# One square of softmax weights per query block: adding the two key blocks of a sliding window before the transposes and parting them with a mask behind

## The chip, the cores and the metric

The kernel runs on one core of a Trainium2 chip. A core has a matrix engine (TensorE, called PE in the profile, with its weight loads on a line of their own, PEld), a vector engine (VectorE, DVE), an engine for activation functions (ScalarE, ACT), a general engine (GpSimd, POOL), and a queue engine (SyncE, SP) that issues most of the DMA transfers here. The metric is the time of one execution on the device in microseconds (us); less is better.

## What is computed

The program is a decoder of two layers on 512 tokens of width 1024, in float32. Layer A has latent attention with 8 heads, layer B has attention in a sliding window of 128 tokens with 16 query heads and 4 key/value heads. Each layer ends with an MLP of width 4096 with a squared ReLU, and both halves end in a layer norm. The part that the change touches is the mixer of layer B:

```python
def _swa(x, w_q, sinks, w_o, k_band, v_band, rel_bias):
    q = (x @ w_q).reshape(B, nb, BLOCK, SWA_KV_HEADS, G, SWA_HEAD_DIM)
    s = jnp.einsum('bnqkgd,bnjkd->bnkgqj', q, k_band).astype(jnp.float32) * SWA_HEAD_DIM ** -0.5
    i = jnp.arange(BLOCK)
    j = jnp.arange(2 * BLOCK)
    dist = i[:, None] + BLOCK - j[None, :]
    ...
    valid = (dist >= 0) & (dist < WINDOW)
    ...
    s = jnp.where(mask[None, :, None, None], s + bias, -jnp.inf)
    ...
    p = jnp.exp(s - m[..., None])
    denom = p.sum(-1) + jnp.exp(sink - m)
    p = (p / denom[..., None]).astype(x.dtype)
    o = jnp.einsum('bnkgqj,bnjkd->bnqkgd', p, v_band).reshape(B, S, SWA_Q_HEADS * SWA_HEAD_DIM)
    return o @ w_o
```

A block of 128 queries sees two blocks of keys, the one before it and its own. With the window of 128, query i of a block sees of its own block the keys up to i, and of the block before the keys after i. So of each pair (query, position in a block) exactly one of the two key blocks has a weight, and the other has zero. The first query block has no block before it.

## The kernel before

Every float32 product is made from two parts: `split` copies a tile to a rounded high part (ACT) and subtracts that from the tile for a low part (DVE, or POOL where the call says so), and matrix products add the terms high by high, high by low and low by high. `group` issues matmuls into one PSUM bank; `bank()` takes one of six banks under the tag `mm`, and `tbank()` one of two under `tr` for transposes. `pe(...)` pins an instruction to the order of the program on its engine; all matmuls and transposes are pinned, so PE's order is that of the code. The other engines' instructions are ordered by the framework's scheduler ahead of the run, and each engine then works through its list in that order. A tile with a tag and `bufs=n` shares n rooms with the other tiles of the tag; a new one waits until an old one has been read for the last time.

Layer B goes through 16 units, one per head, in `run_steps`, with the scores two heads ahead (`AHEAD_B`). In step u PE is given: the scores of head u + 2, some work of the list `fill` (query projections of later heads, in halves; values of blocks 2 and 3; parts of the output projection), the transposes of head u (`turn`), and the mix of head u - 1 (`mix`). For one head:

- `scores`: 8 matmuls for the four query blocks into two banks; DVE adds the bias and takes the row maxima (L1408) and makes the shift `nb` (L1412).
- `weigh`: ACT makes four exponentials with row sums (L1424) and the sink's (L1428); DVE adds them and takes the reciprocal `ri` (L1429, L1430); POOL multiplies the weights by it, first the 128 columns of query block 0, then the 768 of the other three (L1431, L1433). For heads 12 to 14 `weigh` is put off into `turn`.
- `turn`: seven transposes of 128x128 (L1444 and L1446), four of own key blocks and three of the blocks before, into two banks, and two splits into `pth` and `ptl` (512 and 384 columns).
- `mix`: 8 matmuls into one bank: for each key block the values, 64 high and 64 low columns side by side in `vv`, with the weights of that block's own queries and of the next block's, 256 columns (128 for the last). ACT copies the lower half of the bank (L1477), DVE adds it to the upper one (L1478), and after the second head of a pair the pair's output `o` is split into `oh` and `ol`, the low part on POOL.

POOL also makes the low parts of six of the eight `w_sq` weight tiles and of `w_so` tiles 0, 1, 2, 6 and 7 (`wl`). The pool `gp` has one room, tag `gb`; before the change the last two `w_so` tiles are fetched into it ahead of their use (`fetch_two`).

Of the kernel before, what the change touches and what calls it, by code (L numbers as in the profile page):

```python
# [8 lines left out]
F32 = mybir.dt.float32  # L9
# [39 lines left out]
def build(tc, nc, io, out):  # L49
    with ExitStack() as top:  # L50
# [368 lines left out]

        ident = cp.tile([P, P], F32, name="ident")  # L420
# [537 lines left out]
        with tc.tile_pool(name="mla", bufs=1) as mp:  # L958
# [3 lines left out]
            cmask = const[:, C_MASK : C_MASK + 512]  # L962
            cos = const[:, C_COS : C_COS + 256].rearrange("p (t d) -> p t d", t=NT)
# [263 lines left out]
            def turn(h, i):  # L1227
# [62 lines left out]
        def fetch_two(i):  # L1290
            room = gp.tile([P, 2, 1024], F32, tag="gb", bufs=1, name=nm("raw2"))
            for j in range(2):
                fetchers[i + j](room[:, j, :])

        fetch_two(first_o + 6)
# [11 lines left out]
        with tc.tile_pool(name="swa", bufs=1) as mp:  # L1307
# [13 lines left out]
            vv = mp.tile([P, NT, SKVH, P], F32R, name="vv")  # L1321
            wv = []

            vb = {}

# [12 lines left out]
            def values_out(t):  # L1338
                split(vv[:, t, :, 0:64], vv[:, t, :, 64:P], vb[t].rearrange("p (j d) -> p j d", j=4))
# [43 lines left out]
            pts = [None] * SQH  # L1383
# [36 lines left out]
            def weigh(h, bs, nb, sm, ri):  # L1420
                p = mp.tile([P, NT, 256], F32, tag="p", bufs=3, name=nm("p"))
                for n in range(NT):
                    lo_c = P if n == 0 else 0
                    state["exp"] = nc.scalar.activation(  # L1424
                        p[:, n, lo_c:], bs[n // 2][:, n % 2, lo_c:], AF.Exp, bias=nb[:, n : n + 1],
# [5 lines left out]
                nc.gpsimd.tensor_mul(p[:, 0, P:], p[:, 0, P:], ri[:, 0:1].broadcast_to([P, P]))  # L1431
                rest = ri[:, 1:].unsqueeze(2).broadcast_to([P, NT - 1, 256])
                nc.gpsimd.tensor_mul(p[:, 1:, :], p[:, 1:, :], rest)  # L1433
                ps_of[h] = p

            def turn(h, _):
                p = ps_of[h]
                pth = mp.tile([P, NT, 256], F32R, tag="pth", bufs=2, name=nm("pth"))
                ptl = mp.tile([P, NT, 256], F32R, tag="ptl", bufs=2, name=nm("ptl"))
                for k2 in range(2):  # L1440
                    pt = tbank().rearrange("p (a b) -> p a b", a=2)
                    for a in range(2):
                        kb = 2 * k2 + a
                        pe(nc.tensor.transpose(pt[:, a, 0:P], p[:, kb, P:256], ident))  # L1444
                        if kb + 1 < NT:
                            pe(nc.tensor.transpose(pt[:, a, P:256], p[:, kb + 1, 0:P], ident))  # L1446
                    if k2 == 0:

                        with behind((state["exp"],) if h < 10 else None):
                            split(pth[:, 0:2, :], ptl[:, 0:2, :], pt)  # L1450
                    else:
                        flat = lambda z: z.rearrange("p a b -> p (a b)")
                        c = slice(512, 512 + 384)
                        split(flat(pth)[:, c], flat(ptl)[:, c], flat(pt)[:, 0:384])
                pts[h] = pth, ptl
                if waiting:
                    weigh(*waiting.pop())

            ob = [None] * 8

            def mix(h):
                m, a, j = h // 2, h % 2, h // GRP
                if a == 0:
                    ob[m] = mp.tile([P, S], F32, tag="o", bufs=2, name=nm("o"))
                o = ob[m]
                pth, ptl = pts[h]

                b = bank()
                for kb in range(NT):
# [150 lines left out]
```

## Time and profile before

| | |
|---|---|
| median of 3 runs | 993.04 us (993.04 to 993.51) |
| the profiled execution's own time | 993.19 us |
| its span, first to last instruction | 991.4 us |
| granted clock of TensorE | 0.999 of full speed |
| PE busy in the span | 985.3 us (99%) |
| DVE, ACT, POOL busy | 772.2, 555.1, 222.5 us |
| transposes of layer B's weights | 112 (64 at L1444, 48 at L1446), 549.5 to 626.0 us |

The profile is of one execution. A row of its groups names the line of the code, the engine, the operation, what is written and read (tiles by name, without numbers), the shape as partitions x elements, the count, the busy time in us and the mean of one in ns, and then the idle time of that engine just before these instructions and who ended it. The chain of waits follows the work that ended last back from the end; a piece of it is given with its start, its length and the number of instructions. Most of the kernel's matmuls carry the line of the helper `group` (L105) and most splits those of `split` (L77 for the high part, L81 for the low part), so they are told apart by the tiles.

### The profile page before, as it was taken

Reading aid. Unit: us, or ns where it says so; the run is one execution under the profiler, and the core shown is the slowest. Engines: PE = TensorE matmul, PEld = TensorE weight load, DVE = VectorE, ACT = ScalarE, POOL = GpSimd, SP = SyncE. Lnnn points to the kernel's source line nnn. Section 1 sums busy time; section 2 is a strip of 40 time slices with the busy share of each in tenths; the row PEclk is TensorE's granted clock in tenths of the full one; section 3 lists DMA queues with packets and bytes.
Section 4 is the critical chain, followed back from the end, with each engine's and each line's share of the span. In section 5 each row is a group of like instructions: output and inputs, shape, how many; then the busy total and the mean of one; then the engine's idle time right before and its main releaser. Section 6 shows DMA issues by size and latency. Waiting matters only on the chain.

```text
span 991.4 us, 15829 instructions
## 1 busy us (share of the span) xinstructions
PE 985.3 (99%) x6107; PEld 888.3 (90%) x6107; DVE 772.2 (78%) x1240; ACT 555.1 (56%) x851; POOL 222.5 (22%) x207
## 2 busy tenths in 40 slices
PE   9999999999999999999999999999999999999998
PEld 9888888998899999998898998889998998999986
DVE  6589858989768769786686778798885986898756
ACT  5557644467547547646146789536763663664620
POOL 0231101121312212210002775412121122023000
PEclk9999999999999999999999999999999999999999
DMA  7421236399889978964132213338997896898332
GB/s 262 143 90 43 93 121 201 55 230 219 147 195 231 167 163 232 221 108 147 66 107 96 86 66 139 106 85 145 255 199 123 234 213 117 224 261 146 83 128 85
DMA packets 60678, 149.55 MB, mean 151 GB/s; under 512 B 5259, under 2 KB 10300, under 8 KB 60604
## 3 DMA queue, kind: packets, MB, share of 16 engines
q0 software_dynamic: 24320, 58.73, 33.6%
q1 hardware_dynamic: 36140, 89.56, 26.5%
q8 instruction: 48, 0.79, 0.3%
q10 hardware_dynamic: 144, 0.26, 0.1%
q14 instruction: 26, 0.21, 0.1%
HBM read 146.41 MB, written 4.22 MB: 152 GB/s over the span
## 4 chain that ended last, share of the span: by engine, by line
PE 98%; DVE 1%; ACT 1%; DMA 0%; POOL 0%; issue 0%; DVEq 0%; POOLq 0%
PE mm L105 89%; PE tr L105 5%; PE tr L1236 1%; PE tr L1444 1%; PE tr L740 1%; PE tr L1446 1%; DMA raw<-in_w_qr 0%; PE tr L505 0%; ACT wh L77 0%; POOL wl L81 0%; PE mm L1144 0%; PE tr L1004 0%; DVE wl L81 0%; DVE x L479 0%; ACT vh L77 0%
## 5 line engine op out<-in xcount | busy, mean ns | idle before, releaser
L105 PE MATMUL mm<-wh,fac 128*128 128x512 f32 (+1 forms) x944 | 292.5, 386 | 0.0
L77 ACT ACTIVATE wh<-wq 128x1024 fp32r<-128x1024 f32 x164 | 173.7, 1061 | 185.0 <-PE mm L105 132.7
L81 DVE TENSOR_TENSOR wl<-wq,wh 128x1024 fp32r<-128x1024 f32 x164 | 199.5, 1221 | 67.5 <-ACT wh L77 66.6
L105 PE MATMUL mm<-xth,wh 128*128 128x256 f32 (+1 forms) x928 | 243.4, 290 | 0.0
L105 PE MATMUL mm<-xth,wl 128*128 128x256 f32 (+1 forms) x800 | 233.2, 292 | 0.0
L105 PEld LDWEIGHTS mm<-wh,fac 128*128 128x128 f32 x944 | 176.2, 188 | 35.5 <-DVE fac L81 0.6
L105 PE MATMUL mm<-xtl,wh 128*128 128x256 f32 (+1 forms) x672 | 197.1, 293 | 0.0
L105 PE MATMUL mm<-wl,fac 128*128 128x512 f32 (+1 forms) x472 | 182.3, 386 | 0.0
L105 PEld LDWEIGHTS mm<-xth,wh 128*128 128x128 f32 x928 | 168.6, 192 | 3.2
L105 PEld LDWEIGHTS mm<-xth,wl 128*128 128x128 f32 x800 | 153.2, 192 | 2.6
L77 ACT ACTIVATE wh<-raw 128x1024 fp32r<-128x1024 f32 (+3 forms) x86 | 84.9, 989 | 89.8 <-PE mm L105 61.8
L105 PEld LDWEIGHTS mm<-xtl,wh 128*128 128x128 f32 x672 | 128.7, 192 | 3.0
L204 POOL DMA_DIRECT2D wq<-in_up x64 | 77.6, 1241 | 200.3 <-DVE wl L81 193.0
L105 PEld LDWEIGHTS mm<-wl,fac 128*128 128x128 f32 x472 | 88.8, 188 | 16.6
L81 DVE TENSOR_TENSOR wl<-raw,wh 128x1024 fp32r<-128x1024 f32 (+2 forms) x64 | 75.8, 1193 | 31.3 <-ACT wh L77 31.0
L204 POOL DMA_DIRECT2D wq<-in_down x48 | 42.0, 874 | 189.1 <-DVE wl L81 183.2
L81 POOL TENSOR_TENSOR wl<-raw,wh 128x1024 fp32r<-128x1024 f32 (+2 forms) x22 | 46.8, 2130 | 89.7 <-ACT wh L77 67.2
L105 PE MATMUL mm<-wh,oh 128*128 128x512 f32 x128 | 50.8, 397 | 0.0
L105 PE MATMUL mm<-wl,oh 128*128 128x512 f32 x128 | 50.1, 391 | 0.1
L105 PE MATMUL mm<-wh,ol 128*128 128x512 f32 x128 | 50.1, 392 | 0.0
L441 POOL TENSOR_TENSOR rs<-mv,half 128x1 f32<-128x1 f32 x16 | 8.8, 553 | 168.1 <-DVE mv L486 163.4
L639 DVE TENSOR_TENSOR x<-mm,x 128x512 f32<-128x512 f32 (+1 forms) x49 | 32.9, 675 | 15.7 <-PE mm L105 15.6
(233 smaller groups left out, 1823.8 us busy)
## 6 DMA issues: line engine op xcount, KB each, us to landing
wq<-in_up POOLq DMA_DIRECT2D x64, 512.0 KB, 7.4
wq<-in_down POOLq DMA_DIRECT2D x48, 512.0 KB, 7.1
wq<-in_up SPq DMA_DIRECT2D x32, 512.0 KB, 5.5
raw<-in_down SPq DMA_DIRECT2D x28, 512.0 KB, 6.4
wq<-in_down SPq DMA_DIRECT2D x24, 512.0 KB, 6.3
raw<-in_up SPq DMA_DIRECT2D x16, 512.0 KB, 4.3
raw<-in_w_o SPq DMA_DIRECT2D x8, 512.0 KB, 3.3
raw<-in_w_sq SPq DMA_DIRECT2D x8, 512.0 KB, 3.2
```

Source lines behind the costliest of these rows:

```text
L77: high = nc.scalar.activation(dst_h, src, AF.Copy)
L81: low = (engine or nc.vector).tensor_sub(dst_l, src, f32(dst_h))
L105: pe(nc.tensor.matmul(dst, st, mv, start=first and i == 0, stop=last and i == len(pairs) - 1, **kw))
L204: state["added", key, a, more, jp] = nc.gpsimd.dma_start(half(a, jp), chunk(*more, jp), accum_op=ALU.add)
L441: state["rs"] = nc.gpsimd.tensor_tensor(r, v, half, ALU.pow)
L639: nc.vector.tensor_add(xs[t][:, c], b, xs[t][:, c])
L740: pe(nc.tensor.transpose(pt[:, a, :], xs[t][:, k * P : (k + 1) * P], ident))
L1236: pe(nc.tensor.transpose(pt[:, kb * P : (kb + 1) * P], p[:, kb * P : (kb + 1) * P], ident))
L1444: pe(nc.tensor.transpose(pt[:, a, 0:P], p[:, kb, P:256], ident))
L1446: pe(nc.tensor.transpose(pt[:, a, P:256], p[:, kb + 1, 0:P], ident))
```

## The change

In `weigh` the exponentials are laid out in seven squares of 128 columns, and POOL adds the square of the block before to the own square of query blocks 1 to 3 and then multiplies the four squares by `ri`. `turn` makes four transposes into one bank and one split of 512 columns; then POOL multiplies the high part and DVE the low part of blocks 1 to 3 by a triangular mask `tri`, which leaves the weights of the own block (`pmh`, `pml`). The two heads of a pair lie side by side.

`mix` runs once for a pair. Since the whole square is own plus before, the output of a query block is the values of the block before times the whole square, plus the difference of the own block's values and those before (`dv`) times the masked square. For query blocks 0 and 1 together that is one product with `vv` of block 0, 512 columns wide. In all there are 12 matmuls for a pair, into two banks, and four additions instead of two. `values_out` makes `dv` with three copies, three subtractions and three more splits, and drops the last split of `vv`. The mask is made in layer A from the causal mask: one operation of DVE, one transpose and one copy of ACT.

The masked squares have one room, `gb` of the pool `gp`; the two `w_so` tiles that were fetched there go to a room of the tag `xt`. The part (1, 2) of the output projection moves from step 15 to behind the last transposes. The diff, without the lines that only move:

```diff
+                if (h, i) == (2, 0):
+                    nc.vector.tensor_scalar(causal, cmask[:, 384:512], -1.0, 1.0, ALU.max, ALU.add)
...
+                if (h, i) == (4, 0):
+                    pe(nc.tensor.transpose(pt[:, 384:512], causal, ident))
+                    nc.scalar.activation(tri, pt[:, 384:512], AF.Copy)
...
-            vv = mp.tile([P, NT, SKVH, P], F32R, name="vv")
+            vv, dv = [mp.tile([P, NT - 1, SKVH, P], F32R, name=nm("vv")) for _ in range(2)]
...
             def values_out(t):
-                split(vv[:, t, :, 0:64], vv[:, t, :, 64:P], vb[t].rearrange("p (j d) -> p j d", j=4))
+                heads_of = lambda z: z.rearrange("p (j d) -> p j d", j=4)
+                own = vb[t]
+                if t + 1 < NT:
+                    split(vv[:, t, :, 0:64], vv[:, t, :, 64:P], heads_of(own))
+                    vb[t] = room[t]
+                    nc.scalar.activation(vb[t], own, AF.Copy)
+                if t > 0:
+                    d = room[3]
+                    nc.vector.tensor_sub(d, own, vb[t - 1])
+                    split(dv[:, t - 1, :, 0:64], dv[:, t - 1, :, 64:P], heads_of(d))
...
-                nc.gpsimd.tensor_mul(p[:, 0, P:], p[:, 0, P:], ri[:, 0:1].broadcast_to([P, P]))
-                rest = ri[:, 1:].unsqueeze(2).broadcast_to([P, NT - 1, 256])
-                nc.gpsimd.tensor_mul(p[:, 1:, :], p[:, 1:, :], rest)
+                nc.gpsimd.tensor_add(p[:, 2::2, :], p[:, 2::2, :], p[:, 1::2, :])
+                nc.gpsimd.tensor_mul(p[:, 0::2, :], p[:, 0::2, :], ri.unsqueeze(2).broadcast_to([P, NT, P]))
...
             def turn(h, _):
+                m, a = h // 2, h % 2
                 p = ps_of[h]
...
+                if a == 0:
+                    whole = [mp.tile([P, NT, 2, P], F32R, tag=tag, bufs=2, name=nm(tag)) for tag in ("pth", "ptl")]
+                    part = gp.tile([P, 2, NT, 2, P], F32R, tag="gb", bufs=1, name=nm("pm"))
+                    pts[m] = whole + [part[:, i, 1:] for i in range(2)]
+                pth, ptl, pmh, pml = [z[:, :, a, :] for z in pts[m]]
+                pt = tbank().rearrange("p (a b) -> p a b", a=NT)
+                for n in range(NT):
+                    pe(nc.tensor.transpose(pt[:, n, :], p[:, 2 * n, :], ident))
+                with behind((state["exp"],) if h < 10 else None):
+                    split(pth, ptl, pt)
+                own = tri[:, None, :].broadcast_to([P, NT - 1, P])
+                nc.gpsimd.tensor_mul(pmh, f32(pth[:, 1:, :]), own)
+                nc.vector.tensor_mul(pml, f32(ptl[:, 1:, :]), own)
...
+                for n2 in range(2):
+                    b = bank()
+                    parts = b.rearrange("p (n a q) -> p n a q", n=2, a=2)
+                    n = 2 * n2
+                    if n == 0:
+                        group(b, both(vv[:, 0], pth[:, 0:2], ptl[:, 0:2]), True, False, skip_group_check=True)
+                    else:
+                        for i in range(2):
+                            group(
+                                parts[:, i], both(vv[:, n + i - 1], pth[:, n + i], ptl[:, n + i]),
+                                i == 0, False, skip_group_check=True,
+                            )
+                    for i in range(1 if n == 0 else 0, 2):
+                        group(
+                            parts[:, i], both(dv[:, n + i - 1], pmh[:, n + i - 1], pml[:, n + i - 1]),
+                            False, i == 1, skip_group_check=True,
+                        )
+                    low = mp.tile([64, 2, 2, P], F32, tag="low", bufs=2, name=nm("low"))
+                    nc.scalar.activation(low, parts[hi], AF.Copy)
+                    for a, to in enumerate((lo, hi)):
+                        nc.vector.tensor_add(
+                            o[to, n2, :].rearrange("p (n q) -> p n q", n=2),
+                            parts[lo, :, a, :], low[:, :, a, :],
+                        )
...
-            for t, kp, u in (..., (0, 2, 15), (1, 2, 15), (2, 2, 16)):
+            for t, kp, u in (..., (0, 2, 15), (1, 2, 16), (2, 2, 16)):
...
-            run_steps([(h, 0) for h in range(SQH)], AHEAD_B, scores, turn, mix, fill, 1, 1, [])
+            run_steps([(h, 0) for h in range(SQH)], AHEAD_B, scores, turn, mix, fill, 2, 1, [])
```

With `per` = 2 in the last line, `run_steps` calls `mix` in every second step, after the transposes of an even head, for the pair before it.

More of the change, by code (lines that the diff above doesn't have):

```diff
@@ L1436, in turn @@
             def turn(h, _):
+                m, a = h // 2, h % 2
                 p = ps_of[h]
[L1438 to L1454, printed above, removed]
```

47 lines of the change are left out of this document (19 added, 28 removed).

## The prediction

> **What bounds the kernel now.** I read the page first, then the windows over layer B, then the chain of waits there, and then the groups by shape and the timelines of the engines that the change loads.
>
> ```profile
> span 991.4 us, 15829 instructions
> ...
> PE 985.3 (99%) x6107; PEld 888.3 (90%) x6107; DVE 772.2 (78%) x1240; ACT 555.1 (56%) x851; POOL 222.5 (22%) x207
> ```
>
> TensorE (PE) is busy for 99% of the span, and the chain of waits through layer B, below, is PE's own line from piece to piece. Its order is fixed, so every microsecond (us) of PE work that goes is a gain, and every wait of PE is a loss, one for one. The heads of layer B's attention are turned and mixed from about 550 to 626 us; this is the window of four of them in the middle:
>
> ```profile
> core 0: us, PE busy (x) PEld busy (x) DVE busy (x) ACT busy (x) POOL busy (x), PEclk, DMA share, GB/s
> ...
> 581.20:602.77 21.57, 21.57 (x142) 19.40 (x141) 16.95 (x62) 18.99 (x56) 14.61 (x13) 1.00 0.33 107
> ```
>
> In 21.57 us these four heads take 5.39 us each: PE full, ACT 4.75 us per head, DVE 4.24, POOL 3.65. PE is the limit here too, but the others are far closer to it than the 78, 56 and 22% of the page say.
>
> ```profile
> 550.55 3.69 PE mm L105 x20
> ...
> 586.59 0.11 PE tr L1444
> ...
> 587.35 4.63 PE mm L105 x28
> ...
> 602.77 0.11 PE tr L1444
> ...
> 611.76 1.88 PE mm L105 x16
> 613.63 0.11 PE tr L1444
> ```
>
> On the chain a head is seven transposes in 0.76 us (586.59 to 587.35), 0.109 each, and then matmuls. 28 of these are the mix (8), the next scores (8) and 12 of 512 columns; 16 are mix and scores alone. So the 12 cost 4.63 - 1.88 = 2.75 (0.229 each). 20 are scores and those 12: 3.69 - 2.75 = 0.94 for the scores, and 1.88 - 0.94 = 0.94 for the mix, 0.1175 a matmul, although two of its eight have only 128 columns.
>
> **The change, part by part.**
>
> PE. Three transposes fewer per head: 48 x 0.109 = 5.23 us. The mix of two heads was 16 matmuls, 1.88 us; it becomes 2 of 512 columns and 10 of 256, the same columns in fewer instructions: 2 x 0.229 + 10 x 0.1175 = 1.63. Eight pairs save 2.0. The transpose that turns the mask adds 0.11. PE path: -7.1 us, -0.45 a head, so a head takes 4.94 instead of 5.39 if nobody makes PE wait. The bound below is 5.1, should the matmuls of 128 columns not be the dear ones.
>
> ```profile
> L1433 POOL TENSOR_TENSOR p<-p,ri 128x768 f32<-128x768 f32 x16 | 23.5, 1467 | 0.0
> ...
> L1408 DVE CUSTOM_DVE_ANT_0 mm<-mm,bias 128x256 f32<-128x256 f32 x48 | 20.5, 427 | 1.6
> L81 POOL TENSOR_TENSOR wl<-raw,wh 128x1024 fp32r<-128x1024 f32 x8 | 19.2, 2405 | 5.9 <-PE mm L105 3.0 <-ACT wh L77 2.8
> ...
> L1478 DVE TENSOR_TENSOR o<-mm,low 64x512 f32<-64x512 f32 x16 | 10.9, 680 | 2.3 <-ACT low L1477 2.1
> ...
> L81 POOL TENSOR_TENSOR ol<-o,oh 128x512 fp32r<-128x512 f32 x7 | 9.0, 1285 | 3.6 <-ACT oh L77 3.6
> ...
> L81 DVE TENSOR_TENSOR ptl<-tr,pth 128x384 fp32r<-128x384 f32 x16 | 8.8, 549 | 0.0
> ...
> L1431 POOL TENSOR_TENSOR p<-p,ri 128x128 f32<-128x128 f32 x16 | 6.4, 400 | 26.5 <-DVE ri L1430 15.1 <-PE tr L1446 6.4 <-ACT pth L77 4.0
> ```
>
> These groups of layer B by shape (count, busy us, mean ns of one, idle time before) give the prices on the other engines.
>
> ACT loses the second of two splits a head, of 384 columns, and falls below its 4.75 us. The mix's copies keep their count and size.
>
> POOL. Now 0.40 + 1.47 = 1.87 a head. After: an add of 384, a multiply of 512 by the reciprocal, and a multiply of 384 by the mask. Multiplying by the reciprocal costs (1.467 - 0.400)/640 = 1.67 ns an element; two full operands cost (2.405 - 1.285)/512 = 2.19 ns with 0.165 us fixed. By the dearer rate the add and the mask cost 1.01 each, by the cheaper 0.83; I take 1.01, since both read two full operands like `ol`. With 1.04 for the middle one that is 3.06, +1.19, and POOL needs 3.65 + 1.19 = 4.84 of 4.94 us: it is nearly full where weights are split as well.
>
> DVE. It loses 0.549, and gains `pml`, 384 elements with both operands in SBUF. In PSUM that shape is 0.549, and I take 0.55. The two adds of 64x512 in a pair become four of 64x256, at 0.427 by the 256 row: 1.71 for 1.36, +0.17 a head (bounds 0 and 0.34). Together 4.24 - 0.55 + 0.55 + 0.17 = 4.41, before waits. But a two-operand SBUF instruction of DVE is held up by POOL:
>
> ```profile
> L1429 DVE TENSOR_TENSOR sm<-sm,ri x16: 156/163/1620, 541.2 to 619.5; 128x4 f32<-128x4 f32 x16
> 547.78 1.62 DVE L1429 TENSOR_TENSOR sm<-sm,ri 128x4 f32<-128x4 f32 x1 [1.37 <-ACT ri L1428]
> 546.97 2.41 POOL L81 TENSOR_TENSOR wl<-raw,wh 128x1024 fp32r<-128x1024 f32 x1
> ```
>
> An addition of four columns, 0.163 us in the median, once took 1.62 and ended at 549.40, when POOL's 2.41 us instruction did (549.38). In the old loop this tiny one is DVE's only operation of that kind; `pml` is a second and larger one, beside a POOL that hardly rests. The Trainium skill, SBUF — State Buffer, section "Who interferes with whom", has it as a rule: a DVE instruction with two SBUF inputs and a GpSimd instruction that reads SBUF exclude each other, and the later one blocks. The trace agrees in those three rows.
>
> The values: five more ACT and five more DVE instructions of 256 columns (three copies and three subtractions, with one split less of `vv` and three of `dv`), 2.1 us on DVE by the 0.427 row. Half run before the loop, half in its first step, and `dv` is needed only at the first mix, 8 us later: nothing, or up to 2.1 if that step were full. The mask in layer A is two small operations under PE work: nothing.
>
> Moves. The two loads of 512 KB for `w_so` go to an `xt` room free once the last query has read `x2`; they keep their place on SP's queue and their weights are used only behind the loop: nothing. The part (1,2) behind the last transposes covers the last masks: nothing. The mask's one buffer makes POOL's and DVE's masks of an even head wait for the mix of the pair before, which follows that head's transposes on PE by 1.6 us; behind them queue the next weights on POOL and the next scores' bias on DVE. The split that feeds these masks follows the same transposes, so the wait is at most those 1.6 us, for masks that PE needs only a pair later: nothing.
>
> Where PE will wait. POOL's room is the time from its weights to their transposes:
>
> ```profile
> 596.69 1.47 POOL L1433 TENSOR_TENSOR p<-p,ri 128x768 f32<-128x768 f32 x1
> ...
> 611.89 1.47 POOL L1433 TENSOR_TENSOR p<-p,ri 128x768 f32<-128x768 f32 x1
> ```
>
> Head 10 is weighed by 598.16 and turned at 602.77 (the chain, above): 4.6 us of room. With 4.84 of its own and 0.55 in which `pml` holds it up, POOL loses 5.39 - 4.94 = 0.45 us a head, some 3.6 over heads 2 to 9. The room is just used up: I take 0.6 us of stall. In heads 10 to 13 a PE step is shorter (611.76 to 613.63 is mix and scores alone). There `ol` of heads 6 and 7 must come out between the weights, one such instruction late: 1.2. Head 13 was weighed at 613.36 for transposes at 613.63, 0.27 us of room; from its scores PE now comes 2 x 0.327 + 0.25 = 0.90 sooner, the weighing takes 0.19 more, and half to a whole mask is ahead of it: 0.8 to 1.8, taken as 1.5.
>
> The PSUM banks are the other place:
>
> ```profile
> 577.30 0.27 PE L105 MATMUL mm<-skh,q 128*128 128x128 f32 x1
> ...
> 584.27 0.30 ACT L1428 ACTIVATE ri<-nb,sink 128x4 f32<-128x4 f32 x1
> ```
>
> ```profile
> PEld mm L105 <- ACT p L1424: 0.2, 1, 0.2
> ```
>
> Of six, the scores of two heads need four, the mix now two at once, the queries one or two. A head's scores free theirs 7.0 us after their start (577.30 to 584.27), and PE comes for the next after 0.94 + 2.75 + 0.44 + 1.63 + 0.94 = 6.7: 0.3 a pair, 1.0 in all (bounds 0 and the rival below). In the old trace PE has met this limit once, for 0.2 us, the last row.
>
> Sum, on the profiled execution's 993.19 us (span 991.40, 1.79 around it): 993.19 - 7.1 + 0.6 + 1.2 + 1.5 + 1.0 = 990.4, and 990.2 on the scale of the median, 993.04.
>
> **The rivals.** "All of it": POOL has slack for late splits of weights, and ACT's relief brings the weights earlier; then 993.04 - 7.1 = 985.9. For it: the split of weights is POOL's longest item, and nothing in the groups shows PE waiting for one in this stage. Against: 4.84 of 4.94.
>
> "Banks": the pair's two banks let PE run no faster than before until head 11, so five pairs lose 0.90 each, and head 13 its 1.5: 985.9 + 4.5 + 1.5 = 991.9. For it, the 0.2 us row; against, ACT's lighter queue.
>
> "The shared port", the slower one: `pml` and `sm` come upon a POOL that never rests. Two heads of POOL are six instructions near 1.02, one of 1.285 and one of 2.405, 9.8 us; who comes at random waits for half the sum of squares over that, 13.7/19.6 = 0.70. Two waits a head make DVE 4.41 + 1.4 = 5.81, above the old 5.39: DVE becomes the bound, +0.42 a head. Over heads 2 to 13 that is +5.0, the other four save 1.8: 993.04 + 3.2 = 996.2. It decides from waits of 0.98 a head on. For it, the 1.62; against, that 15 of 16 `sm` waited for nothing with POOL at 68%. The rule of the Trainium skill named above (SBUF — State Buffer, "Who interferes with whom") would make every such meeting a wait, and so speaks for this case; by the old trace's 15 free additions the sum stays at 990.2.
>
> "It does not do what it says", that 128-column matmuls were not dear, costs 2.0 and lies inside the range.
>
> **How the numbers follow.** Measured runs lie within 0.05%; 0.2% (2.0 us) is about what can be told. Forecast 990.2: chance 0.34, its own range 988 to 991. All of it: 0.16. Banks: 0.20, within 0.2%. Shared port: 0.30. So faster 0.50, same 0.20, slower 0.30. The range runs from 985.5 to 998.0, the port's price with waits of 0.77 each (4.41 + 1.54 - 5.39 = 0.56 a head); what is left out is the longer tail of that case and a PE gain above 7.5.
>
> **What would show it.** Right: 64 transposes of layer B's weights where there were 112 (64 + 48), 96 matmuls of the mix where there were 128, POOL's groups near 1.0 us each, POOL above 90% from 560 to 600, `pml` in the median over 0.55 with a tail up to POOL's instructions, and PE idle before the transposes of heads 10 to 13 with POOL as releaser. Wrong: PE without idle (all of it), PE released by ACT's exponentials before scores (banks), or DVE at 95% with waits on it (port). A wait outside layer B would make the whole argument wrong.

## The result, and the profile after

The changed kernel takes 1004.9 us in the median of four runs (1004.07 to 1005.95), against 993.06 for the kernel before on the same chip: a ratio of 1.0119, interval 1.0101 to 1.0136. It is 11.8 us slower. The prediction said 990.2, between 985.5 and 998.0. The profiled execution took 1004.18 us, with a span of 1002.4.

From the page of the changed kernel: the span, the engines, and the chain of waits by engine.

```profile
span 1002.4 us, 15698 instructions
...
PE 986.2 (98%) x6028; PEld 884.4 (88%) x6028; DVE 789.0 (79%) x1262; ACT 549.5 (55%) x841; POOL 245.7 (25%) x223
...
PE 91%; DVE 5%; ACT 2%; issue 1%; POOL 0%; DVEq 0%; ACTq 0%; POOLq 0%
```

PE issues 79 instructions fewer and yet is not free sooner. The chain is no longer PE's own line: DVE carries 5% of it, on lines of layer B's heads. Next come three windows of the changed kernel: the two pairs of heads 6 to 9, from the transposes of head 6 to those of head 10, and then two stretches of pair 0.

```profile
core 0: us, PE busy (x) PEld busy (x) DVE busy (x) ACT busy (x) POOL busy (x), PEclk, DMA share, GB/s
584.49:607.63 23.14, 21.45 (x122) 17.66 (x121) 20.79 (x64) 17.20 (x54) 20.43 (x16) 1.00 0.19 65
558.00:562.70 4.70, 2.08 (x11) 1.22 (x10) 4.42 (x15) 3.94 (x16) 3.48 (x4) 1.00 0.42 159
562.70:566.10 3.40, 3.40 (x18) 3.40 (x17) 2.22 (x6) 3.15 (x6) 3.28 (x3) 0.50 0.00 0
```

Four heads take 23.14 us where they took 21.57, though PE's work in them should have fallen to about 19.8 (4 x 4.94, the prediction's estimate). DVE is busy for 20.79 instead of 16.95, POOL for 20.43 instead of 14.61. Most of DVE's growth lies in two groups, here by their shortest, median and longest instruction:

```profile
L1446 DVE TENSOR_TENSOR sm<-sm,ri x16: 156/856/972, 541.3 to 629.1; 128x4 f32<-128x4 f32 x16
L1467 DVE TENSOR_TENSOR pm<-ptl,tri x16: 553/559/1420, 554.2 to 637.3; 128x384 fp32r<-128x384 f32 x16
```

The addition of the sink, four columns, took 0.163 us in the median before and takes 0.856 now. It is the exception of the old trace become the rule. The timeline of one meeting, from three engines, with PE's wait behind it:

```profile
584.37 0.30 ACT L1445 ACTIVATE ri<-nb,sink 128x4 f32<-128x4 f32 x1
584.56 0.60 ACT L77 ACTIVATE pth<-tr 128x512 fp32r<-128x512 f32 x1
...
584.57 0.99 POOL L1448 TENSOR_TENSOR p<-p 128x384 f32<-128x384 f32 x1 [0.77 <-ACT p L1440]
...
584.71 0.88 DVE L1446 TENSOR_TENSOR sm<-sm,ri 128x4 f32<-128x4 f32 x1 [0.47 <-ACT ri L1445]
585.62 0.18 DVE L1447 RECIPROCAL ri<-sm 128x4 f32<-128x4 f32 x1
585.71 0.66 DVE L81 TENSOR_TENSOR ptl<-tr,pth 128x512 fp32r<-128x512 f32 x1
...
586.43 0.50 PE L105 MATMUL mm<-ptl,vv 128*128 128x512 f32 x1 [0.72 <-DVE ptl L81]
```

The last exponential of the weights releases POOL's new addition of the blocks (L1448), and the sink's, right behind it on ACT (L1445), releases DVE's addition of the sink (L1446). POOL starts 0.14 us sooner, and DVE is through only when POOL is (585.59 against 585.56). The odd head's low part `ptl` stands behind that on DVE, and its high part `pth` stands on ACT behind those exponentials; the mix of the pair wants both, and PE stands for 0.72 us. The Trainium skill, SBUF — State Buffer, section "Who interferes with whom", calls this an exclusive lock of a shared port, not a slowdown; the rows agree, 0.88 us for work of 0.16.

The sink's addition of the next head, 2.4 us later, is blocked by another POOL instruction, the multiplication by the reciprocal. In the same meeting PE's weight loads show what one mix costs:

```profile
586.47 1.39 POOL L1449 TENSOR_TENSOR p<-p,ri 128x512 f32<-128x512 f32 x1
587.10 0.79 DVE L1446 TENSOR_TENSOR sm<-sm,ri 128x4 f32<-128x4 f32 x1
```

```profile
585.21 0.19 PEld L105 LDWEIGHTS mm<-pth,vv 128*128 128x128 f32 x1 [0.36 <-ACT pth L77]
586.42 0.19 PEld L105 LDWEIGHTS mm<-ptl,vv 128*128 128x128 f32 x1 [1.03 <-DVE ptl L81]
...
587.02 0.19 PEld L105 LDWEIGHTS mm<-pm,vv 128*128 128x128 f32 x1 [0.26 <-DVE pm L1467]
```

The three waits, for the odd head's high part, its low part and its low mask, add up to 1.65 us. In the timelines, 9 of the 16 additions of the sink end with POOL's new addition, three with its multiplication, one with a split of weights and one with the high mask, and two are free.

What PE waits for over the whole stage, in the list of waits, and the last two waits in its timeline:

```profile
PE mm L105 <- DVE ptl L81: 3.7, 5, 0.8
PE mm L105 <- ACT p L1440: 2.0, 1, 2.0
PE tr L1462 <- POOL p L1449: 1.5, 1, 1.5
PE mm L105 <- ACT pth L77: 1.2, 2, 1.0
PE mm L105 <- DVE pm L1467: 0.8, 1, 0.8
PE mm L105 <- DVE o L1499: 0.6, 1, 0.6
```

```profile
620.70 0.58 PE L105 MATMUL mm<-pth,vv 128*128 128x256 f32 x1 [1.98 <-ACT p L1440]
625.87 0.66 PE L1462 MATMUL tr<-ident,p 128*128 128x128 f32 x4 [1.49 <-POOL p L1449]
```

Against PE's work alone, by the starts of the transposes, the stage loses 5.0 us at pair 0, 1.7 at each of pairs 1 to 4 (6.7), and 6.3 between the transposes of head 11 and those of head 13: 18.0. Less the 7.1 that PE's work gained, that is 10.9 of the 11.0 by which the span grew. About 1.7 of the 5.0 and 1.7 of the 6.3 are not waits but stretches at half the clock; the last section has them. At pair 0 the exponentials of head 3 are late, because DVE was held twice in the split of a difference of values (1.39 and 1.34, named `vv` in the trace) while POOL split weights, and once in the low mask (1.36) while POOL made the high one; `pth` of head 1 stands behind them, and then `ptl` and the mask come one by one.

### The profile page after: what moved, and what is told of

Same layout as the page of the kernel before. It is cut to its first block, busy times and chain, and to the rows that moved or that the text cites. A ratio compares the mean times of both kernels' runs of the same rounds, so it can differ in the third digit from the quotient of the medians.

```text
span 1002.4 us, 15698 instructions
## 1 busy us (share of the span) xinstructions
PE 986.2 (98%) x6028; PEld 884.4 (88%) x6028; DVE 789.0 (79%) x1262; ACT 549.5 (55%) x841; POOL 245.7 (25%) x223
## 4 chain that ended last, share of the span: by engine, by line
PE 91%; DVE 5%; ACT 2%; issue 1%; POOL 0%; DVEq 0%; ACTq 0%; POOLq 0%
PE mm L105 84%; PE tr L105 5%; ACT p L1440 2%; DVE mm L1424 1%; PE tr L1240 1%; PE tr L741 1%; DVE sm L1446 1%; DVE ptl L81 1%; DVE q L1396 1%; DVE pm L1467 1%; DVE o L1499 1%; PE tr L506 0%; POOL wl L81 0%; PE tr L1006 0%; DVE vv L81 0%
```

## The experiments

Three theories ran through them. **Port**: DVE, blocked by POOL, sets the pace. **Pair**, later called **chain**: the mix of two heads follows too soon behind the odd head's split, and the split hangs on the exponentials, these on DVE, and DVE on the mix before. **Banks**: six PSUM banks are too few once a mix takes two. A run's ratio is to the kernel before on the same chip, whose median lay between 992.86 and 993.19 in all of them. What a run loses is counted from that median; what it gives back is counted from the changed kernel's 1004.9, which was measured with another set of runs, so tenths of a microsecond mean little there.

**The sink's sum with one operand in PSUM.** It takes away the blocking of that addition.

```diff
-                nc.scalar.activation(ri, nb, AF.Exp, bias=sink[:, h : h + 1])
-                nc.vector.tensor_add(sm, sm, ri)
+                own_sink = bs[0][:, 0, NT : 2 * NT]
+                nc.scalar.activation(own_sink, nb, AF.Exp, bias=sink[:, h : h + 1])
+                nc.vector.tensor_add(sm, own_sink, sm)
```

> The sink's exponential goes to a free corner of the scores' PSUM bank, so that DVE's addition of four columns reads one operand from SBUF instead of two; nothing else changes. Theory port (DVE sets the pace, and loses about 0.7 us a head because POOL's new addition starts just when DVE adds the sink): that addition falls from 0.86 us in the median to about 0.2, a pair of heads from 11.57 us to about 10.3, and the kernel from 1004.9 to about 997. Theory pair (PE waits for the odd head's weights because the mix of a pair follows too soon behind the split, whatever DVE does in between): the addition gets as short, the time falls by 2 us at most. A third one, banks: the corner is held until the addition is done, and if PE waits for banks the time rises.

Measured 1006.45, ratio 1.0133 (1.0118 to 1.0148). The line of the addition, and what PE's weight loads waited for:

```profile
L1447 DVE TENSOR_TENSOR sm<-mm,sm x16: 150/156/163, 541.2 to 631.9; 128x4 f32<-128x4 f32 x16
...
PEld mm L105 <- DVE sm L1447: 8.4, 5, 2.0
```

With one operand in PSUM all 16 additions are free, also one at 590.29 that lies within a split of weights on POOL (588.91 to 591.27): the blocking is of two SBUF operands, as the rule of the Trainium skill named above has it. But the scores' bank is now held until DVE comes to the sum, and PE waits for that bank, its weight loads for 8.4 us in five places. The blocking is real; what was saved went to the banks.

**No low mask.** The product of the difference reads the unmasked low part.

```diff
-                nc.vector.tensor_mul(pml, f32(ptl[:, 1:, :]), own)
...
-  both(dv[:, n + i - 1], pmh[:, n + i - 1], pml[:, n + i - 1])
+  both(dv[:, n + i - 1], pmh[:, n + i - 1], ptl[:, n + i])
```

> Leaves out DVE's multiplication of the low part by the mask; the mix reads the unmasked low part in its place, with as many matmuls. Theory port: DVE is rid of 0.74 us a head and POOL's multiply of 1.39 us goes back to 1.04, so a pair takes 10.2 us or less, the kernel 992 to 997. Theory pair: only the wait for this one product goes, about 0.3 us a pair, and with the first pair's 1.0 the kernel is 1001 to 1003.

Measured 999.98, ratio 1.0072 (1.0057 to 1.0087): 4.9 us back, for an instruction of 0.56 us a head in the median. That lies between the ranges of the two theories.

**The old arithmetic, mixed in pairs.** The kernel before, with `mix` of both heads behind the next even head's transposes, a third room for the split weights, and the `w_so` tiles moved as in the change.

```diff
+            def mix_two(h):
+                mix(h - 1)
+                mix(h)
...
-            run_steps([(h, 0) for h in range(SQH)], AHEAD_B, scores, turn, mix, fill, 1, 1, [])
+            run_steps([(h, 0) for h in range(SQH)], AHEAD_B, scores, turn, mix_two, fill, 2, 1, [])
```

> The kernel before, with its seven transposes and two splits a head, but with the two heads of a pair mixed in one go behind the transposes of the next even head, as after the change; the third room for weights is the gb room, and the two w_so tiles go to an xt room as after the change. Theory port: no new two-operand work, so 993 to 994, no change. Theory pair: PE waits before each mix for the odd head's second split, 1 us or more a pair, 1000 or more.

Measured 998.97, ratio 1.0059 (1.0042 to 1.0076). The four heads from 5 on, in its windows:

```profile
576.98:600.54 23.56, 22.03 (x142) 19.37 (x140) 17.77 (x61) 18.89 (x56) 14.15 (x13) 1.00 0.20 68
```

With not a mask nor an addition on POOL, and no engine but PE near full, the pairing, with the moves of rooms that it needs, costs 6.1 us, half of the loss. PE's list names two waits: transposes for the splits that still read their banks (2.6 us) and matmuls for exponentials (1.9). The prediction had 1.0 us for the banks of a pair, and no term for how soon its mix follows the odd head's split.

**The mix one head later.** The changed kernel with the last argument but one of `run_steps` (the lag) 2 for 1.

> The changed kernel with the mix of a pair one step later, behind the transposes of the next odd head (lag 2 instead of 1). Theory pair: the odd head's low part and masks have a whole step of some 4 us more, PE's wait of 1.6 us a pair goes, the kernel 988 to 994. Theory port: DVE and POOL have as much to do as before and PE only waits elsewhere, 1001 to 1005. The masks' single room delays the masks of the next even head by one step, which costs something if POOL then falls behind.

Measured 1002.26, ratio 1.0097 (1.0082 to 1.0112). PE no longer waits for `ptl`, but for exponentials (3.3 us), `q` (2.6), `o` (2.2) and POOL's weights (1.8): a gain of 2.6, the rest turned into other waits. The time is in the range of the port theory.

**One head a mix.** The square and the masks, but `mix` for one head and one bank: 2 matmuls of 256 columns and 10 of 128.

```diff
+                group(b[:, 0:256], both(vv[:, 0], pth[:, 0:2], ptl[:, 0:2]), True, False, ...)
+                for n in range(2, NT):
+                    group(parts[:, n], both(vv[:, n - 1], pth[:, n], ptl[:, n]), False, False, ...)
+                for n in range(1, NT):
+                    group(parts[:, n], both(dv[:, n - 1], pmh[:, n - 1], pml[:, n - 1]), False, n == NT - 1, ...)
...
-            run_steps(..., 2, 1, [])
+            run_steps(..., 1, 1, [])
```

> The square, the masks and both POOL instructions as in the changed kernel, but each head is mixed by itself behind the next head's transposes, as before (one bank a mix, 2 matmuls of 256 columns and 10 of 128). PE's sum: 48 transposes less are -5.2; if a matmul of 128 columns costs the 0.1175 of one of 256, a mix is 12 x 0.1175 = 1.41 against 0.94, +7.5 in all, so 993.1 + 2.4 = 995.4 with no wait; if it costs half, 0.82, so 986. Pair theory (the loss comes from mixing two heads at once, too close behind the odd head's split): the wait for ptl before a mix is gone, and the time is that sum, 995 to 997 or 986 to 988. Port theory (DVE and POOL block each other and DVE sets the pace): the sink's addition stays near 0.85 us and DVE stays at 10.4 of 12 us or more, 1000 or more. Banks theory (six PSUM banks are too few for two at once): as the pair theory, and no wait of PE for exponentials before scores.

Measured 1005.24, ratio 1.0123 (1.0106 to 1.014). PE's timeline has such a mix from 588.29 to 589.67, 1.38 us: a matmul of 128 columns is as dear here as one of 256. So the work alone would have given 995.4, and 10 us were lost all the same. The longest of PE's waits, 3.6 of 7.0 us in its list, is now the one for the low mask:

```profile
PE mm L105 <- DVE pm L1468: 3.6, 4, 0.9
PE mm L105 <- DVE vv L81: 1.9, 1, 1.9
```

The pair theory falls as the sole cause. A mix right behind the transposes, of one head too, waits for the mask.

**A bank of the transposes for the mix.** `b = tbank() if n2 else bank()`.

> The changed kernel, but the second of a mix's two banks is one of the two that the transposes use, so the scores and queries have one more of the six. Banks theory: the waits of PE for ACT's exponentials and for the additions into o before matmuls (2.0 and 0.6 us) go, and the scores of the next head start earlier: 1001 to 1002.5. Pair theory and port theory: the mix still waits 0.5 to 0.8 us for the low part of the odd head in each pair; 1003.5 to 1005.5.

Measured 1005.72, ratio 1.0125 (1.011 to 1.014): nothing. The wait of the mix's second bank for exponentials (2.0 us) is gone from PE's list, as the banks theory had it, but the one for POOL's weights grew from 1.5 to 2.9 and the one for `o` from 0.6 to 1.3, and `ptl` is as late as before (3.7).

**The sink's sum on POOL.** `nc.gpsimd.tensor_add(sm, sm, ri)` ahead of POOL's addition of the blocks.

> The changed kernel, but the sink's addition sm <- sm + ri is done by POOL ahead of its add of the blocks, so that DVE no longer meets POOL there, and no PSUM bank is held for it. Port theory: DVE loses 16 x 0.85 us and its blocked time, about 0.7 us a head net; pair period 11.57 falls to near 10.8; 998 to 1001. Pair theory: the odd head's split stands behind the exponentials of a later head, and these do not come sooner by more than what DVE gains; 1001 to 1004. Banks theory: the banks come free when the exponentials are done, as now; 1003.5 to 1005.5.

Measured 1007.3, ratio 1.0141 (1.0125 to 1.0156), slower, against all three. On POOL the sink's addition takes 0.20 us, but PE's one wait for POOL's weights grew from 1.5 to 3.4.

**No masks at all.**

> The changed kernel with neither mask: the difference product reads the unmasked weights, so the later key block's share is counted for queries outside the mask. PE's work stays. It is 0.55 us of DVE and 1.04 us of POOL less a head. Without the low mask alone it was 999.98. Port theory: POOL has a quarter less to do and DVE is blocked less; PE runs nearly free, 988 to 993. Pair theory: the mix still stands behind the odd head's low part (wait 0.2 to 0.5 a pair instead of 0.5 to 0.8), the old algebra in pairs lost 6 us without any mask; 996 to 1000. Banks theory: waits of PE before scores and queries remain, 995 to 999.

Measured 998.3, ratio 1.0055 (1.004 to 1.007). Its window over four heads, from head 5 on:

```profile
576.84:600.15 23.31, 21.00 (x122) 17.63 (x120) 19.70 (x61) 17.19 (x52) 15.30 (x12) 1.00 0.20 69
```

The 6.6 us that it gains lie at the start and the end. In the middle it is as slow as the changed kernel, 23.31 against 23.14, with POOL at 66% and DVE at 85%: no engine is full. What runs there is a ring, and the chain theory is what its timeline suggests, though no run shows each of its links: the mix, its additions into `o` on DVE, the bias and maxima of the next scores behind them, the exponentials, the blocked `sm`, the split, the mix.

**Breaking the ring.** Two edges were taken out, the order that queues the split behind the exponentials, and then `sm` on POOL as well.

```diff
-                with behind((state["exp"],) if h < 10 else None):
-                    split(pth, ptl, pt)
+                split(pth, ptl, pt)
```

> The changed kernel without the order that queues the split of a turned head behind the latest exponentials (heads 0 to 9), so ACT and DVE may split it as soon as it is turned. Chain theory (a pair's mix waits for the odd head's split, this for the exponentials of the head two later, these for DVE's additions into o of the mix before: a ring of 11.6 us a pair that no engine's own work fills): the waits for ptl and pth before a mix go (0.7 in pairs 1 to 4, 2.6 in pair 0), pair period 10.8 or less; 997 to 1000. Port theory (DVE with its blocked time sets the pace, 10.6 busy of 12): 1002 to 1005, with other waits in the place of these. Banks theory: scores wait for exponentials that now come 0.6 later, 1004 to 1007.

> The changed kernel without that order and with the sink's addition on POOL. Chain theory: the split no longer hangs on the exponentials, and DVE sheds about 0.7 us a head; period between 9.9 and 10.4 a pair, 994 to 998, that is 2 to 4 less than with the free split alone. Port theory: only the addition on POOL helps, 1000 to 1003. Banks theory: 1004 to 1007.

The free split alone gives 1004.01, ratio 1.0109 (1.0091 to 1.0128), no more than 0.9 us; the sum on POOL alone had lost 2.4; both together give 998.44, ratio 1.0051 (1.0035 to 1.0067), 6.5 us back. The windows over four heads are for the sum on POOL alone (from head 6), then the free split alone, then both (from head 5; the changed kernel takes 23.10 there):

```profile
584.78:608.01 23.23, 21.86 (x121) 17.68 (x120) 20.00 (x60) 16.80 (x51) 20.74 (x20) 1.00 0.17 60
```

```profile
580.22:603.88 23.66, 21.13 (x121) 17.61 (x120) 20.88 (x61) 17.53 (x52) 22.01 (x17) 1.00 0.19 68
```

```profile
579.75:600.95 21.20, 20.60 (x121) 17.63 (x120) 17.42 (x58) 16.31 (x48) 19.25 (x21) 1.00 0.16 60
```

23.23 and 23.66 became 21.20. That the two effects do not add up is shown. That either edge alone was enough to hold the ring is the reading of it that fits best. The chain theory had forecast 997 to 1000 for the free split alone and missed it by 4 us; for both edits it had 994 to 998 and just missed. DVE also fell from 20.00 and 20.88 us to 17.42 in these windows, so the port theory could claim a part of the gain.

**The pairing again, without that order.** The old arithmetic in pairs, its first split free.

> The kernel before, with two heads mixed behind one another as in the experiment with the old algebra (998.97), now without the order that queues the split's first half behind the exponentials. Chain theory: the waits of 1.0 us a pair for that split go, period from 11.78 to 10.8 (PE's own 10.78); 993 to 995. Port theory: the pairs themselves bring nothing to POOL or DVE, so nothing but the order can have cost the 6 us: the same, 993 to 995. Banks theory: the pair's two banks stay, 997 to 1000.

Measured 998.79, ratio 1.0058 (1.0042 to 1.0074), the same as with the order. Here the forecasts of the chain and the port theory are wrong and that of the banks theory is right. PE waits twice for exponentials (1.9 us) and three times, in the middle of an odd head's step, for the bank that DVE's `q` holds (1.0 us in PE's list; where it stands for 0.35 the scores take 1.65 us instead of 0.94). These are 2.9 of the 5.6 us lost; the rest was not traced.

**POOL's addition alone.** The kernel before with one POOL addition of 128x384 right behind the exponentials, its result unused.

```diff
+                extra = mp.tile([P, NT - 1, P], F32, tag="extra", bufs=1, name=nm("extra"))
+                nc.gpsimd.tensor_add(extra, p[:, 1:, 0:P], p[:, 1:, P:256])
```

> The kernel before with one more POOL instruction a head, an addition of the two blocks (128x384) into a scratch room right behind the exponentials, ahead of the weighing; its result is not used. It puts POOL's new addition by itself into the old loop. Port theory: the sink's addition on DVE rises from 0.163 in the median to near 0.85, since the exponentials release both at once; DVE 4.24 + 0.7 of 5.39 us a head still fits, so 993 to 995, POOL 4.65 of 5.39. Chain theory: the same figures; a time over 996 would show that POOL's longer way to the weights alone costs it (POOL's room before the transposes was 4.6 us at head 10 and 0.27 at head 13).

Measured 995.91, ratio 1.0027 (1.0016 to 1.0037). The sink's sum in its lines, and what the weight loads of PE waited for:

```profile
L1429 DVE TENSOR_TENSOR sm<-sm,ri x16: 399/734/1548, 541.7 to 622.5; 128x4 f32<-128x4 f32 x16
...
PEld tr L1446 <- POOL p L1433: 2.0, 4, 0.5
```

One instruction on POOL lifts an addition on DVE, another engine's, from 0.163 to 0.734 in the median, all 16 of them; 13 of them end with the new instruction. By the longer way to the weights it makes the transposes late: 2.7 us in all, just above the port theory's range. The prediction had terms for POOL's late weights, but none for what this addition does to DVE's.

**What is left when the parts are taken away together.** Free split and sum on POOL in all of these; in the first three also the bank of the transposes; the low mask left out in all but the first and the last; and the mix one head later in three.

> The changed kernel with the free split, the sink's addition on POOL (these two together gave 998.44) and the second bank of a mix taken from the two of the transposes. Banks theory: of PE's waits left, 3.6 us are for exponentials before scores, that is for banks; they go: 995 to 997. Chain theory: the exponentials are late because DVE gives them their maxima late, and a freed bank moves the wait to the next transposes or the mix: 997.5 to 999.5.

> As the run before (free split, sum on POOL, bank of the transposes), and the low mask is left out: the low part of the difference product keeps the later block's weights outside the mask. DVE loses 0.55 us a head and what POOL blocks of it (0.94 in the mean, with the sum on POOL). Chain and port theories: DVE falls to some 3.7 us a head and PE is held only by POOL (10.1 of a pair's 9.9): 990 to 994, so near or under the kernel before. If the pairing itself were a cost that no engine's load explains, 995 or more.

> The same without the low mask, and each pair mixed one head later. Chain theory: POOL's mask of the odd head gets a whole head's time, the wait for it goes, but p and the banks are held longer: 989 to 993, within 2 of the run before. Banks theory: slower than the run before by 2 to 4, since the mix's two banks meet the next head's scores.

> The free split, the sum on POOL and no low mask, with the pair mixed as in the changed kernel and all its banks from the six. With the transposes' bank it was 996.24, of which 5 us were one wait for POOL's weighing of one head. Chain theory: 993 to 996; banks theory: 997 or more, since scores wait for exponentials as in the run with the mask (3.6 us of 998.44).

> The changed kernel with the free split, the sum on POOL, no low mask and each pair mixed one head later, with the mix's second bank again from the six (the run with it from the transposes' two gave 993.79, and its transposes waited 2.4 us for the mix's bank). If the transposes' bank was the brake: 990 to 992.5, faster than the kernel before. Banks theory: the six are again too few for scores of two heads, two of a mix and the queries: 994 to 997.

> All the arithmetic of the changed kernel, both masks, with the free split, the sum on POOL and each pair mixed one head later. With the mix behind the next even head it was 998.44. Chain theory: what is left there are waits for the low mask and the exponentials; a head's time more for the masks brings 2 to 4: 994 to 997. Port theory: DVE with its blocked low mask sets the pace, 997 to 999.

| free split and sum on POOL, and | us | ratio to before (interval) |
|---|---|---|
| bank of the transposes | 1002.87 | 1.0101 (1.0086 to 1.0116) |
| bank, no low mask | 996.24 | 1.0034 (1.0021 to 1.0047) |
| bank, no low mask, mix later | 993.79 | 1.0009 (1.0 to 1.0019) |
| no low mask | 993.18 | 1.0002 (0.9993 to 1.001) |
| no low mask, mix later | 994.42 | 1.0018 (1.0009 to 1.0026) |
| mix later | 998.32 | 1.0059 (1.0046 to 1.0073) |

The bank theory's help again does not come: with the bank of the transposes the first is 4.4 slower than without, for PE's transposes then wait for POOL's weights (3.9 us in three places). With the ring broken the low mask is worth 5.3 us (998.44 to 993.18), or 3.9 with the mix later. By their forecasts the table is no clean win for one theory: without the low mask (993.18) it is the chain's, with the mix later (998.32) the port's, without the low mask and with the mix later (994.42) the banks'. The second (996.24) is in the range for a cost of the pairing itself, but PE waited 4.5 us in one place for POOL's weights there. The first and the third lie outside all ranges given for them. The best, at 993.18, is level with the kernel before and has not beaten it. Its window over four heads from head 5 on, and that of the run with bank, no low mask and later mix:

```profile
575.78:596.89 21.11, 20.56 (x122) 17.64 (x120) 15.85 (x56) 17.66 (x53) 20.93 (x21) 1.00 0.21 76
```

```profile
573.05:593.24 20.19, 20.03 (x121) 17.39 (x120) 15.54 (x59) 18.01 (x55) 19.43 (x20) 1.00 0.22 80
```

In the first POOL is busy for 20.93 of 21.11 us. In the second PE is at 20.03 of 20.19, four heads in 5.05 each: there the gain that the prediction promised is there, 1.4 us under the old 21.57. From head 6 to head 10 the same run takes 21.21, and heads 10 to 13 lose the rest: it waits twice for POOL's weights (0.87 and 1.04) and once for the transposes' bank that the mix borrows and that the split into `ptl` still reads (2.44).

## Why the prediction was wrong

**PE's work: right.** 64 transposes, 12 matmuls a pair, 6028 PE instructions for 6107. Where nothing waits, in the run with the bank and no low mask, PE's timeline shows the transposes of three heads at

```profile
585.66 0.60 PE L1462 MATMUL tr<-ident,p 128*128 128x128 f32 x4
...
589.80 0.60 PE L1462 MATMUL tr<-ident,p 128*128 128x128 f32 x4
...
595.58 0.60 PE L1462 MATMUL tr<-ident,p 128*128 128x128 f32 x4
```

9.92 us for a pair, 4.96 a head; forecast 4.94.

**POOL's prices: right, its share wrong.** From the groups of the changed kernel:

```profile
L1449 POOL TENSOR_TENSOR p<-p,ri 128x512 f32<-128x512 f32 x16 | 20.2, 1263 | 2.1 <-DVE ri L1447 2.0
L1466 POOL TENSOR_TENSOR pm<-pth,tri 128x384 fp32r<-128x384 f32 x16 | 16.7, 1042 | 3.3 <-ACT pth L77 2.3 <-PE mm L105 0.7 <-POOL p L1448 0.3
L1448 POOL TENSOR_TENSOR p<-p 128x384 f32<-128x384 f32 x16 | 16.1, 1007 | 14.7 <-ACT p L1440 14.7
...
L1499 DVE TENSOR_TENSOR o<-mm,low 64x256 f32<-64x256 f32 x32 | 13.3, 415 | 2.8 <-ACT low L1497 2.4
```

1.01 for the addition and 1.04 for the mask against 1.01 each, and 1.26 for the multiplication against 1.04. Without the low mask on DVE the multiplication takes 1.04 in the median, so the rest is the low mask that holds it up, as the prediction had said. POOL above 90% from 560 to 600 did not show: it was busy for 32.77 of these 40 us, 82%, in a loop that had slowed.

**The failed steps** are the places that were put at nothing or near it.

First, "masks that PE needs only a pair later: nothing". True of the even head. The odd head's split and masks are needed by the very next mix, behind one step of PE's work without a mix, and the split is queued on ACT behind the exponentials of the head two later. The old loop gave a head's split a step with a mix as well, and nobody waited. That pairing costs 6 us in the old arithmetic too, where PE's list names PSUM banks that the odd head's splits and the scores hold; the changed kernel's 1.7 at every mix of pairs 1 to 4 is the same closeness, with the odd head's parts and mask as the releasers.

Second, the port. The prediction read the one blocked addition rightly, weighed it against 15 free ones, and asked how often two unrelated instructions meet. But the change makes the end of the exponentials release both POOL's addition and DVE's, and keeps POOL busy at most other times: 14 of 16 are blocked, 0.856 in the median. The rival "The shared port" had the blocking right and nearly the pace: 5.81 us a head, against 5.79 measured (23.14 / 4). That it came so near is luck: it made DVE the bound, and DVE was busy for 90% of the window, under the 95% named as its sign, while without both masks the middle was no faster. Its 996.2 was still 8.7 too low, since it left the first pair and the last heads as they were.

Third, "Half run before the loop ... nothing, or up to 2.1" for the values. It priced them by a row that reads PSUM, but the splits of the differences read two operands in SBUF, and the blocking that the prediction named for `sm` and `pml` holds for them too: two of them, of 256 columns, took 1.39 and 1.34 us instead of 0.43, behind POOL's splits of weights, and pair 0 lost 5.0 us. The first of them:

```profile
551.62 2.40 POOL L81 TENSOR_TENSOR wl<-raw,wh 128x1024 fp32r<-128x1024 f32 x1
552.92 1.39 DVE L81 TENSOR_TENSOR vv<-vf,vv 128x256 fp32r<-128x256 f32 x1
```

**The size of the waits.** 0.6 for POOL's share and 1.0 for banks over the middle were 6.7 (with pair 0, 11.7); 1.2 and 1.5 for heads 10 to 13 were 6.3, though the one wait named, of head 13 for POOL's weighing, came at 1.49 against a forecast of 1.5. That is luck in part, since its head came some 12 us later than in the kernel before; also, PE stood once for 1.98 us for a bank that exponentials still read. "PE full" as the test of the first bound was sound; what it did not show is how long before its use each input of a mix is ready, and the change moved a mix to where it is not ready in time.

**What stays open.** The parts do not add up: pairing 6.1, POOL's addition 2.7 and both masks 6.6 less PE's 7.1 make 8.3 of 11.8. The rest is in their meeting, and the runs show that one edge hides another but not a sum by cause. In the best version 7.3 us lie between 993.2 and PE's work (985.9); its list of waits names exponentials (1.8) and `ptl` (0.9) first, and POOL's 99% in the middle bounds it, but no run took these away. A kernel that moves some of POOL's work to another engine was not tried.

## What to carry to other kernels

When a change groups the work of two steps into one, list for each input of the grouped step who makes it, how long ago, and what is queued ahead of it on that engine; the busy shares don't show that. When two instructions of DVE and POOL can block each other, ask whether one event releases both, since then they meet nearly every time. A loss that no single undoing gives back may be held by two causes at once: undo them together before giving a cause up.

## What the runs showed of the hardware

The clock of PE fell to half behind waits that were each short. In the windows above PE's granted clock is 1.00 up to 562.70, then 0.50 for 3.4 us, and then full. Before it, for 4.7 us, PE had only a few matmuls between three waits of 0.96, 0.81 and 0.84 us:

```profile
559.55 0.50 PE L105 MATMUL mm<-pth,vv 128*128 128x512 f32 x1 [0.96 <-ACT pth L77]
560.86 0.50 PE L105 MATMUL mm<-ptl,vv 128*128 128x512 f32 x1 [0.81 <-DVE ptl L81]
...
562.32 0.38 PE L105 MATMUL mm<-pm,vv 128*128 128x256 f32 x1 [0.84 <-DVE pm L1467]
```

There is a second fall, behind the wait of 1.98:

```profile
618.70:620.70 2.00, 0.03 (x1) 0.00 (x0) 1.99 (x8) 1.56 (x6) 0.00 (x0) 1.00 0.00 0
620.80:624.20 3.40, 3.40 (x16) 3.38 (x16) 1.54 (x3) 3.40 (x15) 2.30 (x2) 0.51 0.00 0
```

In the 3.4 us before each fall PE was busy for 1.50 and for 1.43 us. In the slow stretch matmuls of 256 columns start 0.21 us apart instead of 0.12. By an estimate, each fall costs about 1.7 us beyond the waits (half of 3.4). The Trainium skill, TensorE: Matmul & The Clock Gate, section "Part 1: The HAM clock gate", has the gate go to half after an idle window of about 3.4 us and back after a busy one. The length of the slow stretch agrees; the fall came here with no idle of that length, the longest being 1.98.

The lock works both ways. With the sink's sum on POOL it is POOL that stands, behind a split of weights on DVE, in the run with the bank and no low mask:

```profile
615.04 1.99 DVE L81 TENSOR_TENSOR wl<-raw,wh 128x1024 fp32r<-128x1024 f32 x1 [0.59 <-ACT wh L77]
...
615.90 1.19 POOL L1446 TENSOR_TENSOR sm<-sm,ri 128x4 f32<-128x4 f32 x1
```

1.19 us for an addition that takes 0.20 us in the median of that run; it ends at 617.09, when DVE has just ended (617.03).
